# Weights' second part written by a negated copy and an adding DMA, in a four-layer mixer kernel on one core

## The chip, the core and the metric

The kernel runs on one core of a Trainium2 chip. The metric is the time of one execution on the device, in microseconds. The engines are named as the profile names them: PE (TensorE) multiplies matrices, PEld is its weight load, DVE (VectorE) and ACT (ScalarE) work elementwise, POOL (GpSimd) does so too and issues DMAs of its own, SP (SyncE) issues most DMAs.

## The reference, cut to what matters

The input is x, 512 tokens of 1024 features, in fp32. Four layers follow each other: a gated convolution of 31 taps beside an RWKV-7 recurrence; attention over keys that an indexer selects; an LRU; an attention with forget gates. Each begins and ends with large products of fp32 weights:

```python
z = h @ even_w_in[j]                      # 1024 x 7296
out = jnp.concatenate([ya, yb], axis=-1) @ even_w_out[j]   # 2048 x 1024
...
z = h @ odd_w_in[j]                       # 1024 x 4936
out = (o * jax.nn.silu(g)) @ odd_w_out[j] # 2048 x 1024
...
u = h @ w_in                              # LRU: 1024 x 3072, out 1536 x 1024
...
u = h @ w_in                              # forget gates: 1024 x 4112, out 1024 x 1024
```

The work between them is smaller on TensorE: the convolution, the recurrence in chunks of 64 tokens, the selection, two softmax attentions, the scan of the LRU.

## The kernel before, in words

Products are kept near fp32 by splitting both operands into two parts of the type fp32r, a first part h (the operand rounded) and a second part l (what rounding left). A product of one row tile (128 rows of the weights) is then three matmuls (`mm3`, L161 to L165): first part by first part (L163), first by second (L164), and the weights' second part by the first part of x (L165).

Weights come by column tiles of 128 columns. `wsplit` (L126) loads 8 row tiles of a column tile, 512 KB, through SP into `wr` (3 buffers), and makes the parts in two halves of 4 row tiles each: ScalarE casts the raw half into `wh` (L138), then GpSimd subtracts `wh` from the raw half into `wl` (L139). `wh` and `wl` have 4 buffers each, so a new half can be made when the half four back has been used. `wrows` (L143) does the same for rows of 7 column tiles in the first layer (L153, L154). In the LRU's output projection a half has 3 row tiles; in the last layer's products by tokens (`project_tok`) a half is one row tile of 512 columns, and two halves are used together. The last weights of all have buffers of their own (tag `pT`).

The convolution's taps are L835, `taps`: 27 products and sums on VectorE for each of 8 feature tiles, with some on GpSimd (L840). The inverse of the recurrence's triangular blocks is L665 and L666, 31 steps of a small product and a sum on VectorE. L870 sums the convolution's squares on GpSimd. The LRU's gates are functions on ScalarE (L1346 to L1361). L1088 is the one place where GpSimd issues DMAs: two copies of the indexer's keys from 64 partitions to the other 64.

The order on each engine is set by a scheduler that simulates the program as it is written; work marked as later is filled in behind. Each engine then works through its own queue in that order.

Of the kernel before, what the change touches and what calls it, by code (L numbers as in the profile page):

```python
# [10 lines left out]
F = mybir.dt.float32  # L11
R = mybir.dt.float32r
# [3 lines left out]
OP = mybir.AluOpType  # L16
# [15 lines left out]
# Columns of the packed vectors: a vector of n floats holds n / 128 columns.  # L32
# [20 lines left out]
class Ctx:  # L53
    """Pools, constants and the steps that the layers share."""
# [17 lines left out]
    @contextlib.contextmanager  # L72
    def layer(self, name, ps, **slots):
        """A pool for one layer's tiles: numbers of buffers by tag; for PSUM the banks, in turn."""
        self.slots, self.banks = slots, {tag: itertools.cycle(b) for tag, b in ps.items()}
        with self.tc.tile_pool(name=name, bufs=1) as self.sb:
            yield
# [6 lines left out]
    def one(self, name, shape, dt=F):  # L84
        """A tile of its own for the layer."""
        return self.sb.tile(list(shape), dt, name=self.name(name))
# [19 lines left out]
    def bias(self, v):  # L106
        """A column that holds v."""
# [17 lines left out]

    def wsplit(self, key, idx, k0, kn, rows=True, tag=None):  # L126
        """Rows k0 to k0 + kn (of 128) of a column tile of weights, each in two parts; or its halves."""
# [8 lines left out]
        for k in range(0, kn, n):  # L136
            h, l = (self.t(tag, (P, 4, P), R) if tag else self.wp.tile([P, 4, P], R, name=self.name(z), tag=z, bufs=4) for z in ("wh", "wl"))
            nc.scalar.copy(h[:, :n], raw[:, k:k + n])  # L138
            nc.gpsimd.tensor_tensor(out=l[:, :n], in0=raw[:, k:k + n], in1=h[:, :n].bitcast(F), op=OP.subtract)  # L139
            out += [(h[:, i], l[:, i]) for i in range(n)] if rows else [[z.rearrange("p a c -> p (a c)") for z in (h, l)]]  # L140
        return out

    def wrows(self, key, ct, k):  # L143
        """Rows k (of 128) of 7 or 8 column tiles, evenly apart, in two parts."""
# [5 lines left out]
        for o in (0, 4):  # L150
            m = min(4, n - o)
            h, l = (self.wp.tile([P, 4, P], R, name=self.name(z), tag=z, bufs=4) for z in ("wh", "wl"))
            nc.scalar.copy(h[:, :m], raw[:, o:o + m])  # L153
            nc.gpsimd.tensor_tensor(out=l[:, :m], in0=raw[:, o:o + m], in1=h[:, :m].bitcast(F), op=OP.subtract)  # L154
# [12 lines left out]
    def project(self, key, ct, xs, evac, group=1, sub=(), first=0, tag="mm"):  # L167
        """Column tiles ct of the weights, from row tile first on, times xs, a list of (h, l) of 128 rows."""
# [16 lines left out]
    def fill(self, key, ct, xs, evac, sub=()):  # L185
        """As project, a step of the sums at a time."""
# [11 lines left out]
    def lead(self, key, ct, xs, evac, tag="mm", sub=()):  # L198
        """As project, of two column tiles at once, a step of the sums of both at a time."""
# [10 lines left out]
    def steps(self, gen, n=None, after=None):  # L210
        """n steps, or all that are left, of work that fills gaps of TensorE: issued after an instruction."""
# [4 lines left out]
    def sums(self, key, ct, v, tag, raw):  # L216
        """Columns: column tiles ct of the weights times the vector v, 1024 long."""
# [17 lines left out]
    def project_halves(self, key, ct, xs, evac, tags, sub=()):  # L235
        """As project, the first half of xs for all column tiles first, then the first tokens: the rest comes later."""
# [15 lines left out]
    def project_tok(self, key, xs, evac, last=None):  # L252
        """xs as the stationary side: the result is by tokens. Weights by halves of the columns. A step at a time.
        last: a tag for the last weights, with which the last columns' blocks of tokens end one after the other."""
# [18 lines left out]
    def split(self, src, tag, scale=None):  # L273
        """src (fp32, SBUF or PSUM), times scale, as two fp32r tiles."""
# [15 lines left out]

    def bcast_tok(self, r, tag, dtag="s"):
        """r: [128 tokens, 4 blocks] -> [128, 512] in PSUM, the same in every partition."""
# [7 lines left out]
    def later(self, *after):  # L300
        """Work that fills gaps: yields to what is traced after it, and is issued after those instructions."""
# [12 lines left out]
    def stack(self, f, out, l=None):  # L314
        """Two heads of 64 rows, each split: both parts in the rows of a tile; or l, and the first part twice."""
# [8 lines left out]
    def shifted(self, f, shift):  # L324
        """f + shift, split."""
# [6 lines left out]
class SumSq:  # L332
    """Sums over the features of (x * g)^2, as the tiles of x come; by tokens in the end."""
# [26 lines left out]
def rms_cols(K, s):  # L360
    """1 / sqrt(s / 1024 + eps) by tokens."""
# [6 lines left out]
def log1p_exp_neg(K, t, bufs):  # L368
    """log(1 + exp(-t)) for t >= 0, by the series of atanh: t is overwritten."""
# [15 lines left out]
# ---------------------------------------------------------------- modulation  # L385


class Ada:
    """silu(c) @ ada_w[l] + ada_b[l], as columns: shift, scale and gate are 8 of them each."""
# [6 lines left out]
    def part(self, j, n, tags, after=None, acc="awa", ps="ada"):  # L396
        """Columns of 128, n of them from j on: returns what ends the sums."""
# [22 lines left out]
    def scale(self, j, n=4):  # L420
        """The norm's weight times 1 + scale, n columns."""
# [3 lines left out]
    def columns(self, i, tag):  # L425
        """Columns i and i + 1 of the shift and of the scale."""
# [21 lines left out]
# ---------------------------------------------------------------- layer 0: convolution and RWKV-7  # L448


def even_layer(K, ada1):
# [12 lines left out]
    with K.layer("even", {"mm": (0, 1), "t": (2, 3, 4), "u": (5, 6), "ada": (7,), "py": (7,)}, s=6, k=4, v=4, q4=3, no=1, Yt=1, BKt=2, SAV=2, U=3, cu=2, fg=3, mean=2, awa=1, pa=1):  # L464
# [11 lines left out]
        # a column tile of each kind, as the rows of h come  # L476
# [30 lines left out]
        # sigmoid(z) = (tanh(z / 2) + 1) / 2  # L507
# [3 lines left out]
        # the convolution is of 2 val sigmoid(glu): its norm undoes the 2  # L511
# [12 lines left out]
        def lora(ft, j):  # L524
            """tanh of half of the low-rank sums: 0 the decay's, 1 a's."""
# [6 lines left out]
        def head_sums(sqs, f, n=S):  # L532
            """f of the sums over each head's features, of 4 tiles of n tokens: [two parts of 8 heads, n]."""
# [20 lines left out]
        class Half:  # L554
            """8 heads."""
# [1074 lines left out]
```

## Time and profile before

| | us |
|---|---|
| runs | 1833.74, 1842.38, 1839.56 |
| median | 1839.56 |
| span of the profiled execution | 1835.4 |
| PE busy | 1685.5 (92%) |
| DVE busy | 1319.1 (72%) |
| ACT busy | 899.9 (49%) |
| POOL busy | 866.9 (47%) |
| DMA engines | 30.1% of the span for SP's queue, 1.1% for ACT's, 0.1% for POOL's |

The span runs from the first instruction to the last; what lies around it in that execution is not shown by the profile. Busy time is the time in which at least one instruction of an engine ran; matmuls overlap each other, so a busy PE may still be able to start them more closely. "Idle before" is the engine's idle time just ahead of an instruction, with the instruction that ended it.

### The profile page before, as it was taken

How to read it: one execution, taken by the hardware profiler on the slowest of the kernel's cores; microseconds unless marked ns; L12 is line 12 of the kernel's file. 1: busy time of each engine (PE TensorE's matmuls, PEld its weight loads, DVE VectorE, ACT ScalarE, POOL GpSimd, SP SyncE). 2: the span in 40 equal slices, each digit the busy share in tenths (PEclk: the TensorE clock that was granted, in tenths of full speed). 3: DMA queues.
4: the chain of work that ended last, by engine and by line, in shares of the span. 5: the costliest groups of instructions: out<-in, count | busy, mean ns of one | idle time of the engine just before them, and what ended most of it. 6: DMA issues, size and time to landing. Idle time of an engine off the chain costs nothing.

```text
span 1835.4 us, 25614 instructions
## 1 busy us (share of the span) xinstructions
PE 1685.5 (92%) x9250; PEld 1311.0 (71%) x9250; DVE 1319.1 (72%) x2246; ACT 899.9 (49%) x1699; POOL 866.9 (47%) x682
## 2 busy tenths in 40 slices
PE   3997889999895999898999999999988899999998
PEld 2765678776664777765778788888766687776776
DVE  6689997897969786568969978734898721455552
ACT  2443234334333524466344677644767633555564
POOL 4555564444585422354435555344544443444343
PEclk9997898998988889999999999999999999999999
DMA  9412352214243852331225310022222233321211
GB/s 271 131 58 69 118 144 72 83 47 135 78 126 120 266 185 97 97 99 58 92 86 169 119 53 13 24 92 92 81 89 66 78 103 108 104 81 61 81 55 70
DMA packets 111055, 182.15 MB, mean 99 GB/s; under 512 B 37296, under 2 KB 57136, under 8 KB 110928
## 3 DMA queue, kind: packets, MB, share of 16 engines
q1 hardware_dynamic: 106736, 172.91, 30.1%
q10 hardware_dynamic: 4032, 7.34, 1.1%
q8 instruction: 73, 1.20, 0.3%
q14 instruction: 54, 0.44, 0.1%
q0 software_dynamic: 160, 0.26, 0.1%
HBM read 162.10 MB, written 18.12 MB: 98 GB/s over the span
## 4 chain that ended last, share of the span: by engine, by line
PE 58%; DVE 32%; ACT 4%; issue 4%; DMA 2%; SPq 0%; POOL 0%; DVEq 0%; ACTq 0%
PE ps L163 15%; PE ps L164 15%; PE ps L165 14%; DVE x L835 7%; DVE q L665 2%; DVE xc L1300 2%; DVE q L666 2%; PE ps L1494 1%; DVE SAV L438 1%; DVE u L1369 1%; PE ps L706 1%; PE ps L1477 1%; PE ps L1490 1%; PE ps L1238 1%; PE ps L538 1%
## 5 line engine op out<-in xcount | busy, mean ns | idle before, releaser
L139 POOL TENSOR_TENSOR wl<-wr,wh 128x512 fp32r<-128x512 f32 (+1 forms) x400 | 563.6, 1413 | 657.1 <-ACT wh L138 614.3
L163 PE MATMUL ps<-h,wh 128*128 128x512 f32 x1240 | 511.2, 416 | 31.2 <-DVE s L516 13.2
L165 PE MATMUL ps<-h,wl 128*128 128x512 f32 x1240 | 505.7, 408 | 6.0 <-POOL wl L139 6.0
L164 PE MATMUL ps<-h,wh 128*128 128x512 f32 x1240 | 506.2, 408 | 3.2 <-DVE h L328 2.7
L138 ACT CAST wh<-wr 128x512 fp32r<-128x512 f32 (+1 forms) x400 | 242.0, 609 | 409.4 <-PE ps L164 332.4
L163 PEld LDWEIGHTS ps<-h,wh 128*128 128x128 f32 x1240 | 244.5, 197 | 98.8 <-DVE s L516 17.0
L165 PEld LDWEIGHTS ps<-h,wl 128*128 128x128 f32 x1240 | 243.5, 196 | 63.0 <-POOL wl L139 7.1
L164 PEld LDWEIGHTS ps<-h,wh 128*128 128x128 f32 x1240 | 244.0, 197 | 57.2 <-issue 3.6
L835 DVE SCALAR_TENSOR_TENSOR x<-cu,vec,x 128x512 f32<-128x512 f32 x216 | 214.5, 995 | 4.7
L1235 POOL TENSOR_SCALAR pp<-pp,st 128x512 f32<-128x512 f32 x32 | 52.3, 1634 | 51.9 <-DVE st L1231 38.3
L1484 DVE CUSTOM_DVE_ANT_0 pp<-ps,nb 128x128 f32<-128x128 f32 (+3 forms) x64 | 30.8, 488 | 42.4 <-PE ps L1479 31.2
L1230 ACT ACTIVATE pp<-pp,st 128x512 f32<-128x512 f32 x64 | 46.3, 723 | 23.8 <-DVE st L1229 23.6
L665 DVE TENSOR_TENSOR q<-q,q 128x112 f32<-128x112 f32 (+25 forms) x108 | 46.1, 461 | 15.0 <-POOL q L657 11.7
L1487 POOL TENSOR_SCALAR pp<-pp,st 128x128 f32<-128x128 f32 (+1 forms) x32 | 31.4, 986 | 47.9 <-DVE st L1486 47.8
L1229 DVE CUSTOM_DVE_ANT_0 pp<-ps,bias 128x512 f32<-128x512 f32 x64 | 43.4, 679 | 6.2 <-PE ps L1238 4.2
L164 PE MATMUL ps<-wl,h 128*128 128x512 f32 x120 | 47.2, 393 | 0.0
L1485 ACT ACTIVATE pp<-pp,st 128x128 f32<-128x128 f32 (+3 forms) x64 | 35.9, 561 | 21.8 <-DVE st L1484 21.3
L163 PE MATMUL ps<-wh,h 128*128 128x512 f32 x120 | 46.5, 403 | 0.0
L165 PE MATMUL ps<-wh,h 128*128 128x512 f32 x120 | 46.5, 393 | 0.0
L1491 ACT COPY pT<-ps 128x128 f32<-128x128 f32 (+3 forms) x64 | 26.6, 423 | 39.6 <-PE ps L1490 38.8
L284 DVE TENSOR_TENSOR pT<-ps,pT 128x512 fp32r<-128x512 f32 x64 | 43.4, 680 | 2.3 <-ACT pT L283 2.1
L283 ACT CAST pT<-ps 128x512 fp32r<-128x512 f32 x64 | 36.6, 577 | 16.2 <-PE ps L1238 15.7
(522 smaller groups left out, 3480.7 us busy)
## 6 DMA issues: line engine op xcount, KB each, us to landing
wr<-in_even_w_in SPq DMA_DIRECT2D x50, 512.0 KB, 3.5
wr<-in_odd_w_in SPq DMA_DIRECT2D x39, 512.0 KB, 3.5
wr<-in_lru_w_in SPq DMA_DIRECT2D x24, 512.0 KB, 3.4
wr<-in_fox_w_qkg SPq DMA_DIRECT2D x24, 512.0 KB, 3.5
k<-in_ada_w SPq DMA_DIRECT2D x32, 256.0 KB, 3.0
wr<-in_odd_w_out SPq DMA_DIRECT2D x16, 512.0 KB, 3.8
wr<-in_lru_w_out SPq DMA_DIRECT2D x16, 384.0 KB, 3.1
AR<-in_ada_w SPq DMA_DIRECT2D x4, 1024.0 KB, 9.8
```

Of the source, the lines that this page charges most:

```text
L138: nc.scalar.copy(h[:, :n], raw[:, k:k + n])
L139: nc.gpsimd.tensor_tensor(out=l[:, :n], in0=raw[:, k:k + n], in1=h[:, :n].bitcast(F), op=OP.subtract)
L163: mm(ps, lhsT=w[0], rhs=x[0], start=first, stop=False)
L164: mm(ps, lhsT=w[0], rhs=x[1], start=False, stop=False)
L165: self.last_mm = mm(ps, lhsT=w[1], rhs=x[0], start=False, stop=last).ins
L284: nc.vector.tensor_tensor(out=l, in0=src, in1=h.bitcast(F), op=OP.subtract)
L665: eng.tensor_tensor(out=z, in0=Yu[:, a, b:b + 1].to_broadcast(sh), in1=Nu[:, b:b + 1, b + 1:].to_broadcast(sh), op=OP.mult)
L666: eng.tensor_tensor(out=Yu[:, a, b + 1:], in0=Yu[:, a, b + 1:], in1=z, op=OP.add)
L835: nc.vector.scalar_tensor_tensor(out=acc, in0=u[:, q:q + S], scalar=w[q], in1=acc, op0=OP.mult, op1=OP.add)
L1229: nc.vector.tensor_tensor_reduce(out=pp, in0=lg, in1=bias[t], scale=1.0, scalar=3e38, op0=OP.add, op1=OP.min, accum_out=mx)
L1230: nc.scalar.activation(pp, pp, AF.Exp, scale=-1.0, bias=mx, accum_out=sm)
L1235: (nc.vector if t % 2 else nc.gpsimd).tensor_scalar(out=pp, in0=pp, scalar1=sm, scalar2=None, op0=OP.mult)
```

## The change

A half's second part is no longer subtracted by GpSimd. ScalarE writes the raw half a second time, times -1, into `wl`, which rounds it to fp32r as the first part was rounded; then a DMA from GpSimd's queue adds the raw half to it, in SBUF. `wl` then holds the raw value less the first part, as before. Both `wsplit` and `wrows` call the new function. 418 halves are made in this way (400 by L139 and 16 by L154 before, and 2 with the tag `pT`). The small weights of the LRU's gates (L1339) and the split of activations stay as they were. Comments and docstrings are dropped elsewhere, by which lines after L157 have a number higher by 5.

```diff
-            h, l = (self.t(tag, (P, 4, P), R) if tag else self.wp.tile([P, 4, P], R, name=self.name(z), tag=z, bufs=4) for z in ("wh", "wl"))
-            nc.scalar.copy(h[:, :n], raw[:, k:k + n])
-            nc.gpsimd.tensor_tensor(out=l[:, :n], in0=raw[:, k:k + n], in1=h[:, :n].bitcast(F), op=OP.subtract)
+            h, l = self.wparts(raw[:, k:k + n], tag)
...
+    def wparts(self, raw, tag=None):
+
+        nc, n = self.nc, raw.shape[1]
+        h, l = ((self.t(tag, (P, 4, P), R) if tag else self.wp.tile([P, 4, P], R, name=self.name(z), tag=z, bufs=4))[:, :n] for z in ("wh", "wl"))
+        nc.scalar.copy(h, raw)
+        nc.scalar.mul(l, raw, -1.0)
+        nc.gpsimd.dma_start(out=l, in_=raw, accum_op=OP.add)
+        return h, l
...
-            h, l = (self.wp.tile([P, 4, P], R, name=self.name(z), tag=z, bufs=4) for z in ("wh", "wl"))
-            nc.scalar.copy(h[:, :m], raw[:, o:o + m])
-            nc.gpsimd.tensor_tensor(out=l[:, :m], in0=raw[:, o:o + m], in1=h[:, :m].bitcast(F), op=OP.subtract)
+            h, l = self.wparts(raw[:, o:o + m])
```

GpSimd's queue where the convolution's squares are summed (`mean`, L870, L875 after the change) and the recurrence's inverse begins on VectorE; `wl`, `wh` and `wr` are the parts and the raw weights. Before:

```order
L870 TENSOR_TENSOR mean_4337<-mean_4337,cu_4348 128x512
L139 TENSOR_TENSOR wl_4492<-wr_4485,wh_4491 128x512
L870 TENSOR_TENSOR mean_4337<-mean_4337,cu_4352 128x512
L139 TENSOR_TENSOR wl_4527<-wr_4524,wh_4526 128x512
L870 TENSOR_TENSOR mean_4337<-mean_4337,cu_4356 128x512
L139 TENSOR_TENSOR wl_4531<-wr_4524,wh_4530 128x512
```

And after the change:

```order
L875 TENSOR_TENSOR mean_4441<-mean_4441,cu_4452 128x512
L147 DMA wl_4603<-wr_4595 128x512
L875 TENSOR_TENSOR mean_4441<-mean_4441,cu_4456 128x512
L147 DMA wl_4639<-wr_4636 128x512
L875 TENSOR_TENSOR mean_4441<-mean_4441,cu_4460 128x512
L147 DMA wl_4644<-wr_4636 128x512
```

Each subtraction has become a DMA in the same place; the sums between them have not moved.

ScalarE's queue in the LRU, between the functions of two feature tiles (L1346 to L1353 before, L1351 to L1358 after; `ri`, `u` and `m` are the gates' values). Before:

```order
L138 CAST wh_11841<-wr_11835 128x512
L138 CAST wh_11909<-wr_11907 128x512
L1346 ACTIVATE ri_11623<-ps_11619,hb_11425 128x512
L1338 CAST wah_11883<-wax_11881 128x256
L1346 ACTIVATE ri_11629<-ps_11625,hb_11425 128x512
L1351 ACTIVATE u_11631<-ri_11623,sp_11393 128x512
L283 CAST xs_11721<-xc_11714 128x512
L1352 ACTIVATE ri_11623<-ri_11623,sp_11394 128x512
L138 CAST wh_11913<-wr_11907 128x512
L1353 ACTIVATE m_11632<-ri_11623 128x512
```

And after the change:

```order
L1351 ACTIVATE ri_11891<-ps_11887,hb_11687 128x512
L1343 CAST wah_12159<-wax_12157 128x256
L1351 ACTIVATE ri_11897<-ps_11893,hb_11687 128x512
L145 CAST wh_12185<-wr_12183 128x512
L1356 ACTIVATE u_11899<-ri_11891,sp_11655 128x512
L146 ACTIVATE wl_12186<-wr_12183 128x512
L288 CAST xs_11993<-xc_11986 128x512
L1357 ACTIVATE ri_11891<-ri_11891,sp_11656 128x512
L145 CAST wh_12190<-wr_12183 128x512
L146 ACTIVATE wl_12191<-wr_12183 128x512
L1366 ACTIVATE g_12059<-f_12060 128x512
L1358 ACTIVATE m_11900<-ri_11891 128x512
```

A product (L146) follows each cast (L145) by one place or two, so it stands between the gates' functions where there was nothing or a cast alone.

## Rows read from the trace of the kernel before

**Rows 1.** Page, busy us (share of span) xinstructions.

```profile
PE 1685.5 (92%) x9250; PEld 1311.0 (71%) x9250; DVE 1319.1 (72%) x2246; ACT 899.9 (49%) x1699; POOL 866.9 (47%) x682
```

**Rows 2.** Page, costliest groups: busy, mean ns | idle before, releaser.

```profile
L139 POOL TENSOR_TENSOR wl<-wr,wh 128x512 fp32r<-128x512 f32 (+1 forms) x400 | 563.6, 1413 | 657.1 <-ACT wh L138 614.3
...
L138 ACT CAST wh<-wr 128x512 fp32r<-128x512 f32 (+1 forms) x400 | 242.0, 609 | 409.4 <-PE ps L164 332.4
...
L835 DVE SCALAR_TENSOR_TENSOR x<-cu,vec,x 128x512 f32<-128x512 f32 x216 | 214.5, 995 | 4.7
```

**Rows 3.** Chain of waits, 548 to 566 us: start, us, what.

```profile
548.73 0.23 PE ps L163
```

**Rows 4.** Timeline, ScalarE's casts, 549 to 556 us.

```profile
551.94 0.62 ACT L138 CAST wh<-wr 128x512 fp32r<-128x512 f32 x1 [0.50 <-PE ps L164]
...
554.66 0.63 ACT L138 CAST wh<-wr 128x512 fp32r<-128x512 f32 x1 [0.71 <-PE ps L164]
```

**Rows 5.** Waits: us in total, times, longest us.

```profile
ACT wh L138 <- PE ps L164: 332.4, 177, 10.0
...
PE ps L165 <- POOL wl L139: 6.3, 3, 5.4
```

**Rows 6.** Windows: busy us of each engine, granted clock, DMA share, GB/s.

```profile
0.00:50.00 50.00, 21.92 (x76) 16.72 (x76) 34.55 (x48) 13.51 (x22) 24.62 (x24) 1.00 0.92 278
450.00:500.00 50.00, 44.70 (x156) 31.67 (x157) 48.24 (x51) 20.50 (x33) 28.86 (x23) 0.87 0.32 95
1400.00:1450.00 50.00, 44.14 (x187) 34.08 (x185) 39.88 (x45) 36.40 (x56) 19.87 (x18) 1.00 0.20 59
1500.00:1550.00 50.00, 50.00 (x238) 39.84 (x238) 12.00 (x36) 17.58 (x29) 20.64 (x17) 1.00 0.33 109
```

**Rows 7.** Chain of waits, taps, 460 to 480 us.

```profile
466.55 0.76 DVE x L835
...
467.33 1.67 DVE x L835
```

**Rows 8.** Line L835: count, ns min/median/max, first and last start.

```profile
L835 DVE SCALAR_TENSOR_TENSOR x<-cu,vec,x x216: 721/752/1826, 83.0 to 516.6; 128x512 f32<-128x512 f32 x108
```

**Rows 9.** Timeline, GpSimd in the same stretch.

```profile
468.40 1.74 POOL L139 TENSOR_TENSOR wl<-wr,wh 128x512 fp32r<-128x512 f32 x1
```

**Rows 10.** Chain of waits, the inverse's start, 548 to 566 us.

```profile
549.59 13.81 DVE q L665 x2
```

**Rows 11.** Timeline, GpSimd beside it.

```profile
549.48 1.29 POOL L870 TENSOR_TENSOR mean<-mean,cu 128x512 f32<-128x512 f32 x1
550.73 1.30 POOL L139 TENSOR_TENSOR wl<-wr,wh 128x512 fp32r<-128x512 f32 x1
```

**Rows 12.** Chain of waits, first and last of the 120 long pieces.

```profile
21.09 1.65 DVE SAV L438
...
1451.72 1.33 DVE u L1370
```

**Rows 13.** Line L286: a tile times a number, as fp32r.

```profile
L286 ACT ACTIVATE qs<-s x16: 617/632/649, 849.3 to 1149.9; 128x512 fp32r<-128x512 f32 x16
```

**Rows 14.** Tile ki: GpSimd's DMAs, issue ns and landing us.

```profile
L1088 POOL DMA_DIRECT2D ki<-ki x2: 517/632/747, 805.7 to 806.9; - x2
...
DMA to landing us min/median/max: 2.2/2.3/2.4
```

**Rows 15.** Timeline, 803 to 812 us: GpSimd's issue and VectorE beside it.

```profile
805.73 0.75 POOL L1088 DMA_DIRECT2D ki<-ki  x1 [2.87 <-ACT ki L283]
...
805.96 0.68 DVE L284 TENSOR_TENSOR ki<-s,ki 64x512 fp32r<-64x512 f32 x1
```

**Rows 16.** Page, DMA queues: packets, MB, share of 16 engines.

```profile
q10 hardware_dynamic: 4032, 7.34, 1.1%
...
q0 software_dynamic: 160, 0.26, 0.1%
```

**Rows 17.** Windows, line L139 alone.

```profile
1500.00:1550.00 50.00, 20.64 (x17) 1.00 0.33 109
```

## The prediction

> **What bounds the kernel now.** I read the page's shares first: PE is busy 92% of the span [rows 1]. Then the groups of lines: some 400 weight halves are prepared by a ScalarE cast of 609 ns and a GpSimd subtraction of 1413 ns [rows 2]. A half is four row tiles, so 12 matmuls; where the weights stream, TensorE starts one each 0.23 us [rows 3] and the casts follow each other 2.72 us apart (551.94, 554.66) [rows 4]: 12 x 0.23 = 2.76 us is one half's time. That is the pace any new way of making a half has to keep. The waits say that preparation is not late today: the casts wait 332.4 us for TensorE to free a first-part buffer, and TensorE waits 6.3 us for a second part [rows 5].
>
> Where TensorE is not the bound, VectorE is: 48.24 of 50 us in 450 to 500, with PE at 44.70 [rows 6]. The chain of waits shows why. One convolution tap takes 0.76 us, the next one of the same shape 1.67 [rows 7]; over all 216 taps the least is 721 ns, the median 752, the most 1826 [rows 8]: two kinds, not a spread. In the same microseconds GpSimd ran a subtraction of 1.74 us [rows 9] against a mean of 1413. Two engines that read two SBUF operands each take turns. The extreme case is at 549.59, where two small products last 13.81 us [rows 10] while GpSimd goes from one operation to the next without a gap [rows 11]. Laying GpSimd's timeline beside the chain, I count 120 pieces of VectorE that run over 0.2 us longer than their undisturbed twins (0.72 to 0.76 us for a whole tile) while a weight subtraction is GpSimd's main work: the first at 21.09, the last at 1451.72 [rows 12]. Their excess adds up to 123 us of the chain, 13 of it from [rows 10].
>
> **The change part by part.**
> *Removed:* 400 subtractions, 563.6 us of GpSimd [rows 2], and 16 like them in the first 75 us. The end does not wait for GpSimd's time as such; what counts is the 123 us of turns on the chain. Not all come back. GpSimd's other operations also read SBUF (L870 alternates with L139 in [rows 11]) and keep their turns, and in 450 to 500 TensorE has only 50 - 44.70 = 5.3 us idle to give, although its low starts there can close up too. Ends: 0 and 123; I take 55, a little under half.
>
> *Added on ScalarE:* 418 products with -1. The row nearest is a whole tile times a number, written as fp32r: 632 ns [rows 13]. 418 x 0.63 = 264 us, so ScalarE goes from 49% to about 63%. In a stream that is 0.62 + 0.63 of 2.76 us, beside TensorE. It costs where ScalarE is full: in 1400 to 1450 it is busy 36.40 us [rows 6], with some 15 halves 36.4 + 15 x 0.63 = 46 of 50. The order there puts the products between the gates' functions; each such function is late by up to 0.63 us, and the product waits one matmul longer (0.23) for its buffer than the cast did. Ends 0 and 20 us; I take 5.
>
> *Added on GpSimd's queue:* 418 DMAs. The only ones that the trace has move 64 rows of 2 KB: 517 to 747 ns to issue and 2.3 us to landing [rows 14]. 128 rows and a second operand may make it two to four times as long: 1.0 to 3.0 us, I take 1.5, about what the subtraction took, so GpSimd's queue is as occupied as before and what stands behind a DMA there (L870, L1235) is no later. VectorE's two-operand instruction beside that issue took 0.68 us, undisturbed [rows 15]; so I count no turns for a DMA's issue.
>
> *Landing.* Before, a second part was ready 1.4 us after its cast. Now: 0.63 for the product, then the DMA. From 2.3 us for 128 KB I estimate 3.4 us for 256 KB read twice (2.3 us as the lower end, 6 us under load as the upper). With a wait for ScalarE the path from a freed buffer to a ready one is about 5 us, at worst 8. Four buffers rotate, so a freed one is needed three halves later: 3 x 2.76 = 8.3 us. That is hidden in the column projections. It is not where the rotation is short: the by-token projections use two halves together (16 pairs, 5.5 us apart), and the LRU's output has halves of three row tiles (32, three of them 6.2 us). At 0.5 us a pair and 0.3 us a half that is 18 us; I take 15, between 0 and 40.
>
> *DMA engines.* The ACT queue's row gives a price per packet: 1.1% of 16 x 1835.4 us over 4032 packets is 80 ns at 1.8 KB [rows 16]. One plain DMA of 128 rows has 144 packets by the existing pair (160 for two of 64 rows): 144 x 80 / 16 = 0.72 us of all engines; with two reads for each write 1.44. The software queue's own row, 0.1% (0.05 to 0.15 by rounding) for 160 packets, reaches 275 ns and so 5.0 us. I take 1.44, since the 80 ns come from 4032 packets. In 1500 to 1550 the engines are busy 0.33 [rows 6], 0.91 us a half; 0.91 + 1.44 = 2.35 of 2.76 us. It fits, narrowly. At the start they are at 0.92: 8 DMAs (the parts of the first four loads) at 1.44 us, 11.5 us, do not fit in the 4 us left, of which I charge 5 (0 to 15).
>
> The Trainium skill, "DMA: Bandwidth & Descriptors", section "Anatomy of one DMA — SWDGE (gpsimd) path", states 2.0 us plus the bytes over 436 GB/s. That would be 2.6 us by its figures; the 2.3 us row agrees for 128 KB, and with 2.6 the 15 us for short rotations would go, leaving 1795. Against the change speaks the skill's page "SBUF — State Buffer", section "SBUF: two separate sides": while VectorE runs a mode that takes both ports, GpSimd cannot write descriptors. No row here has a GpSimd DMA beside such an operation; by that rule each could wait one of them out, some tenths of a us, within the landing's ends above.
>
> *Sum:* 55 gained, 5 + 15 + 5 = 25 lost: -30. The profiled execution has a span of 1835.4 us, and no more of its time is shown; 1835.4 - 30 = 1805.4. The three runs' median is 1839.56, 4.2 above that span, so the forecast is **1810 us**.
>
> **Rivals.**
> *A, the accumulating DMA does not keep the pace.* The point: more than 2.76 - 0.91 = 1.85 us of all engines for each. For it: the 5.0 us end, and a margin of only 0.4 us; against it: 80 ns a packet. From 1500 to 1550 there are 17 halves [rows 17]; the stretches like it (850 to 1000, 1200 to 1600) hold, by my estimate at that density or a little under, some 200. At 2.3 us they are 0.45 us short each, 90 us: 1839.6 - 30 + 90 = 1900; at 1.85 and a bit, with lateness alone, 1850; at 3.3 us 0.91 + 3.3 = 4.2 for 2.76, +290, about 2100. The place is TensorE at the third product of a row tile (L165 before, L170 after), which would wait for second parts, with DMA at nine tenths.
> *B, no change.* The turns go, but TensorE was next and the chain moves to it; for it speaks the 92%. Then 123 us shrink to about 25, the charges eat them: 1840 (1830 to 1849).
> *C, the turns come back whole* and the charges are hidden by the buffers: 1839.6 - 85 = 1755. For it: TensorE's starts at 0.23 us leave it more room than its busy share says (156 matmuls in 450 to 500 need 36 us); against it: GpSimd's other operations keep taking turns.
>
> **How the numbers follow.** Forecast (1785 to 1830) 0.44; C and what lies below 1785 0.08; B 0.14; A 0.34, of which 0.12 above 1915. Half a per cent, 9 us, is about what runs of this kernel can tell from no change. Faster 0.52, same 0.14, slower 0.34. The forecast's own range is 1785 to 1830; A's part up to 1915 has to be in the 8 of 10: 1785 to 1915.
>
> **What would show it.** Right: the taps' mean falls from 995 towards 800 ns, and the two products at 549.59 from 13.81 to a few us; ScalarE's busy time is near 1160 us; TensorE's waits for a second part stay below 40 us in all; landing of the new DMAs has a median under 5 us. Wrong: landing above 8 us or an issue above 2.7 us, TensorE idle before that third product by 100 us or more, DMA at 9 tenths in the projections (A); taps as fast as I say with the total unmoved (B).

## The result, and the profile after

The changed kernel takes 1806.72 us (median of four runs, 1806.24 to 1814.26) against 1836.94 for the kernel before, measured beside it: a ratio of 0.9845 with a 95% interval of 0.9817 to 0.9873. The forecast was 1810 us. By the medians the kernel gained 30.2 us, and 30 were forecast; the forecast lies 3 us higher because it was worked out from the 1839.56 us of three runs. The profiled execution is the slowest of the four: 1814.26 us with a span of 1812.5. It is 8 us above the other three, so a stage read from one execution is uncertain by about that much.

The page of the changed kernel: busy time and share of each engine, then three DMA queues (packets, MB, share of 16 engines), then the chain that ended last (the run of work and waits, followed back from the last instruction), by engine; the last row is that chain before the change.

```profile
PE 1684.2 (93%) x9250; PEld 1306.3 (72%) x9250; DVE 1140.0 (63%) x2246; ACT 1102.2 (61%) x2117; POOL 643.0 (35%) x682
...
q0 software_dynamic: 60352, 107.24, 35.0%
q1 hardware_dynamic: 106736, 172.91, 30.8%
q10 hardware_dynamic: 4032, 7.34, 1.1%
...
PE 62%; DVE 13%; DMA 10%; issue 6%; ACT 6%; POOL 2%; SPq 0%; POOLq 0%; ACTq 0%; DVEq 0%
...
PE 58%; DVE 32%; ACT 4%; issue 4%; DMA 2%; SPq 0%; POOL 0%; DVEq 0%; ACTq 0%
```

Beside [rows 1], VectorE lost 179 us of busy time (1319.1 to 1140.0) with the same 2246 instructions. TensorE's busy time stayed (1685.5 to 1684.2). Its idle time, span less busy, fell from 149.9 to 128.3 us: that is nearly all of what the span lost. In the chain VectorE went from 32% to 13% and DMA from 2% to 10%, so a good part of what VectorE gave back went to transfers.

Costliest groups of the changed kernel: busy, mean ns | idle before, releaser.

```profile
L147 POOL DMA_DIRECT2D wl<-wr x416 | 365.9, 887 | 884.9 <-ACT wl L146 771.9
...
L146 ACT ACTIVATE wl<-wr 128x512 fp32r<-128x512 f32 (+1 forms) x416 | 256.6, 617 | 34.9 <-PE ps L169 28.1
L840 DVE SCALAR_TENSOR_TENSOR x<-cu,vec,x 128x512 f32<-128x512 f32 x216 | 178.0, 827 | 4.5
```

A tap takes 827 ns in the mean, 995 in [rows 2]. The next answers are for single lines: count, ns min/median/max, first and last start; for the DMA also its landing; then VectorE's timeline at the place of [rows 10], GpSimd's beside it, and TensorE's behind it.

```profile
L147 POOL DMA_DIRECT2D wl<-wr x416: 830/860/1699, 21.1 to 1792.2; - x139
DMA to landing us min/median/max: 3.0/4.2/8.2
L840 DVE SCALAR_TENSOR_TENSOR x<-cu,vec,x x216: 723/752/2205, 87.6 to 492.1; 128x512 f32<-128x512 f32 x108
...
527.13 0.57 DVE L670 TENSOR_TENSOR q<-q,q 128x31 f32<-128x31 f32 x2 [13.43 <-DMA q<-sp]
...
530.62 13.29 POOL L875 TENSOR_TENSOR mean<-mean,cu 128x512 f32<-128x512 f32 x1
...
548.94 0.80 PE L170 MATMUL ps<-h,wl 128*128 128x512 f32 x1 [10.01 <-DMA wl<-wr]
```

The two small products that lasted 13.81 us now last 0.57. But the collision has not gone: it has turned around. VectorE now goes from one step of the inverse to the next without a gap, and one of GpSimd's sums (L875), 1.29 us long in [rows 11], takes 13.29. The adding DMA behind that sum in GpSimd's queue starts only at 543.85, and TensorE sits idle for 10.01 us until it has landed. The taps still have a largest value of 2205 ns: two taps that begin at 390.54 take 3.13 us together, with two of GpSimd's own operations (L852, L845) beside them, so its other work goes on taking turns with VectorE. Waits of the changed kernel: us in total, times, longest us; the last two rows are of SyncE's queue, which loads the weights, after and before the change.

```profile
PE ps L170 <- DMA wl<-wr: 28.4, 20, 10.0
...
SPq L133 <- DMA wl<-wr: 1204.4, 193, 48.0
...
SPq L133 <- POOL wl L139: 1114.9, 183, 49.9
```

Where [rows 5] had 6.3 us, TensorE's matmuls now wait 28.4 us for a second part; the longest of these waits, 10.0 us, is the one at 548.94. The last rows show something more: a load of weights (L133) now waits until the adding DMA has read the raw tile, where GpSimd's subtraction freed it before. These waits grew by 90 us in all; what that cost isn't shown.

Windows of the changed kernel: busy us of each engine, granted clock, DMA share, GB/s. Then pieces of its chain of waits: start, us, what.

```profile
0.00:50.00 50.00, 18.80 (x74) 15.13 (x75) 32.96 (x48) 16.84 (x29) 17.68 (x23) 1.00 0.96 277
450.00:500.00 50.00, 47.33 (x197) 32.43 (x196) 47.35 (x60) 27.07 (x47) 27.14 (x30) 0.93 0.72 168
540.00:545.00 5.00, 0.00 (x0) 0.00 (x0) 5.00 (x19) 0.00 (x0) 5.00 (x3) 0.84 0.05 4
550.00:600.00 50.00, 43.06 (x386) 33.73 (x385) 25.74 (x36) 29.51 (x51) 18.41 (x19) 0.83 0.99 265
1500.00:1550.00 50.00, 50.00 (x247) 39.95 (x246) 13.23 (x46) 30.25 (x58) 15.00 (x18) 1.00 0.87 204
```

```profile
232.81 7.30 DMA wl<-wr
...
530.62 13.24 POOL mean L875
543.85 5.04 DMA wl<-wr
...
770.54 5.84 DMA wl<-wr
```

In the even stream of 1500 to 1550 TensorE is full beside a DMA share of 0.87. The losses stand elsewhere: at the start, where TensorE is busy for 18.80 us instead of the 21.92 of [rows 6], at 232.81 and in the second layer's input products (770.54). The one at 543.85 is not the work of many transfers: from 540 to 545 TensorE does nothing while the DMA engines' share is 0.05, because the DMA's issue stands behind GpSimd's long sum. The share of 0.99 comes after it.

Where the span goes by stage, from one execution of each kernel. The marks are the first starts of lines 862, 1298 and 1401 of the kernel before (867, 1303 and 1406 after): the convolution's mean, the LRU, the last layer. The experiments e1 and so on come below.

| kernel | to L862 | to L1298 | to L1401 | to the end | span |
|---|---|---|---|---|---|
| before | 528 | 751 | 246 | 310 | 1835.4 |
| after | 504 | 756 | 239 | 314 | 1812.5 |
| e1 GpSimd only writes | 467 | 726 | 224 | 308 | 1724.8 |
| e5 plain DMA, no product | 479 | 735 | 226 | 308 | 1747.1 |
| e3 plain DMA | 479 | 734 | 237 | 309 | 1759.2 |
| e11 e3 and traffic | 501 | 759 | 241 | 309 | 1811.0 |
| e9 e3 and delay | 509 | 756 | 252 | 315 | 1831.4 |

The change gained 24 us before L862 and 7 in the LRU, and lost 5 between and 5 at the end; of these only the 24 is clear of the 8 us between executions.

### The profile page after: what moved, and what is told of

The parts are those of the page before. It is cut to its first block, busy times and chain, and to the rows that moved or that the text cites. A ratio compares the mean times of both kernels' runs of the same rounds, so it can differ in the third digit from the quotient of the medians.

```text
span 1812.5 us, 26549 instructions
## 1 busy us (share of the span) xinstructions
PE 1684.2 (93%) x9250; PEld 1306.3 (72%) x9250; DVE 1140.0 (63%) x2246; ACT 1102.2 (61%) x2117; POOL 643.0 (35%) x682
## 4 chain that ended last, share of the span: by engine, by line
PE 62%; DVE 13%; DMA 10%; issue 6%; ACT 6%; POOL 2%; SPq 0%; POOLq 0%; ACTq 0%; DVEq 0%
PE ps L168 16%; PE ps L170 16%; PE ps L169 16%; DMA wl<-wr 3%; DVE x L840 2%; PE ps L711 1%; DMA adm<-in_ada_w 1%; PE ps L1499 1%; DVE SAV L443 1%; PE ps L1482 1%; ACT wl L146 1%; PE ps L1495 1%; POOL wl L147 1%; PE ps L1243 1%; DMA wr<-in_even_w_in 1%
## 5 line engine op out<-in xcount | busy, mean ns | idle before, releaser
L147 POOL DMA_DIRECT2D wl<-wr x416 | 365.9, 887 | 884.9 <-ACT wl L146 771.9
L170 PE MATMUL ps<-h,wl 128*128 128x512 f32 x1240 | 499.5, 408 | 26.1 <-DMA wl<-wr 25.5
L168 PE MATMUL ps<-h,wh 128*128 128x512 f32 x1240 | 508.2, 414 | 10.3 <-ACT h L288 3.4
L169 PE MATMUL ps<-h,wh 128*128 128x512 f32 x1240 | 497.7, 404 | 0.0
L145 ACT CAST wh<-wr 128x512 fp32r<-128x512 f32 (+1 forms) x416 | 251.8, 605 | 331.3 <-PE ps L169 237.5
L168 PEld LDWEIGHTS ps<-h,wh 128*128 128x128 f32 x1240 | 241.8, 195 | 74.9 <-issue 6.3
L169 PEld LDWEIGHTS ps<-h,wh 128*128 128x128 f32 x1240 | 241.2, 195 | 53.2 <-issue 4.5
L146 ACT ACTIVATE wl<-wr 128x512 fp32r<-128x512 f32 (+1 forms) x416 | 256.6, 617 | 34.9 <-PE ps L169 28.1
L840 DVE SCALAR_TENSOR_TENSOR x<-cu,vec,x 128x512 f32<-128x512 f32 x216 | 178.0, 827 | 4.5
```

What stands on the lines that cost most here:

```text
L145: nc.scalar.copy(h, raw)
L146: nc.scalar.mul(l, raw, -1.0)
L147: nc.gpsimd.dma_start(out=l, in_=raw, accum_op=OP.add)
L168: mm(ps, lhsT=w[0], rhs=x[0], start=first, stop=False)
L169: mm(ps, lhsT=w[0], rhs=x[1], start=False, stop=False)
L170: self.last_mm = mm(ps, lhsT=w[1], rhs=x[0], start=False, stop=last).ins
```

## The experiments

A turn here is the time that VectorE loses to a GpSimd operation beside it. The theory at the start: the turns of GpSimd's subtraction were worth some 55 us, and the new way of making a second part gives back 25. Its rivals: the gain is GpSimd's shorter queue and not the turns; the price is ScalarE's product, or the DMA. Times are medians, with the ratio to the kernel before on the same chip and its interval; that kernel took 1836.9 to 1838.8 us.

**e1, GpSimd only writes** (kernel before; the subtraction is left out at both of its places, the second part is zero).

```diff
-nc.gpsimd.tensor_tensor(out=l[:, :n], in0=raw[:, k:k + n], in1=h[:, :n].bitcast(F), op=OP.subtract)
+for _ in range(3):
+    nc.gpsimd.memset(l[:, :n].bitcast(F), 0.0)
```

> The kernel before, but GpSimd only writes each weight half's second part (three memsets of zero in a row in place of the subtraction; the second part's product is therefore left out of the result). GpSimd stays occupied for about as long (3 x 0.5 us against 1.41), but reads nothing from SBUF; no DMA is added, ScalarE has no second product. Theory of the turns (two engines that read two SBUF operands each alternate): VectorE's taps fall from 995 ns towards 827 or less, VectorE's busy time to about 1140 us as in the changed kernel, and the time to 1836.9 - 50 = about 1787 us, lower than the changed kernel's 1806.7 because nothing of the change's price is paid. Rival, that the gain comes from a shorter stay in GpSimd's queue: no change, 1828 to 1846 us. Rival, that it comes from a new order of the schedule: anything, with VectorE's busy time unmoved at 1319.

Measured: 1724.64 us, 0.9386 [0.9361, 0.9412]. I expected 1787. Page and groups of this kernel:

```profile
PE 1646.8 (95%) x9250; PEld 1292.6 (75%) x9250; DVE 1142.6 (66%) x2246; ACT 902.2 (52%) x1699; POOL 930.6 (54%) x1518
...
L140 POOL MEMSET wl<- 128x512 f32 (+1 forms) x1200 | 621.7, 525 | 519.7 <-PE ps L167 444.3
L837 DVE SCALAR_TENSOR_TENSOR x<-cu,vec,x 128x512 f32<-128x512 f32 x216 | 180.2, 837 | 4.4
```

GpSimd is busier than before (930.6 against 866.9 us), and still 112 us are gone, with the taps at 837 ns. So the queue theory falls: it is the reading, and the turns cost up to twice what I took. One thing else changes in e1: a write waits neither for the load nor for the cast, but for TensorE (the releaser in its row). In e2 the wait for the cast stays.

**e2, one operand read** (kernel before; GpSimd copies the first part, so the second part is not the remainder).

```diff
-nc.gpsimd.tensor_tensor(out=l[:, :n], in0=raw[:, k:k + n], in1=h[:, :n].bitcast(F), op=OP.subtract)
+nc.gpsimd.tensor_copy(l[:, :n], h[:, :n].bitcast(F))
```

> The kernel before, but GpSimd copies the first part to the second part (one SBUF operand read and one write; the subtraction is left out of the result). If any GpSimd operation that reads SBUF makes VectorE's two-operand instructions take turns: VectorE's taps stay near 950 to 1000 ns where they meet, though each turn is shorter if the copy is shorter than 1.41 us (at about 0.8 us the excess falls by 40%), and the time is between 1800 and 1836, about 1815 us. If only two-operand GpSimd operations take turns: taps near 827, as with memsets, about 1787 us.

Measured: 1752.03 us, 0.9551 [0.9525, 0.9577]. I expected about 1815.

```profile
L139 POOL CAST wl<-wh 128x512 fp32r<-128x512 f32 (+1 forms) x400 | 301.2, 755 | 762.6 <-ACT wh L138 703.1
L835 DVE SCALAR_TENSOR_TENSOR x<-cu,vec,x 128x512 f32<-128x512 f32 x216 | 190.6, 884 | 4.6
```

With one operand read the taps stand at 884 ns, between 837 and 995, and 27 of the 112 us come back: one operand makes turns as well, but fewer; the copies also take only 301.2 us of GpSimd where the subtractions took 563.6. The copy waits for its cast as the subtraction did, and still 85 us are gone. So neither e1's earlier writes nor e2's shorter copies can be the whole cause: e2 is without the first, e1 without the second, and what the two have in common is that GpSimd reads less.

**e3, a plain DMA** (changed kernel without the addition: the second part is the raw weights).

```diff
-nc.gpsimd.dma_start(out=l, in_=raw, accum_op=OP.add)
+nc.gpsimd.dma_start(out=l, in_=raw)
```

> The changed kernel, but the DMA copies the raw half over the second part and does not add (the second part is therefore the raw half in the result). It measures what adding costs: two reads for each write. If the price goes by reads: software queue's share 35% falls to about 17%, 0.76 us of all engines each, landing from 4.2 to about 3 us, and of the 22 to 25 us that the change gives back (start 4.6, first layer's output 8.5 and second layer's start 4.5, second layer's attention 7) about half return: 1795 us. If the price of a DMA lies in its descriptors and its fixed latency: share and landing barely move, 1804 to 1809 us.

Measured: 1766.48 us, 0.9631 [0.9588, 0.9675]. Group, landing and queue of this kernel:

```profile
L147 POOL DMA_DIRECT2D wl<-wr x416 | 229.1, 551 | 940.9 <-ACT wl L146 852.8
...
DMA to landing us min/median/max: 2.1/2.7/6.8
...
q0 software_dynamic: 60352, 107.24, 20.2%
```

I expected 1795, or 1804 to 1809. So adding costs 40 us over copying: 0.34 us more to issue, 1.5 us later to land, and 0.67 us more of all 16 engines (35.0% of 1812.5 against 20.2% of 1759.2, over 418 DMAs: 1.52 against 0.85).

**e4, a hybrid** (DMA for the column tiles of the first layer's and the LRU's input products, the subtraction elsewhere).

```diff
+h, l = self.wparts(raw[:, k:k + n], tag, key in ("even_w_in", "lru_w_in_2"))
...
+if dma:
+    nc.scalar.mul(l, raw, -1.0)
+    nc.gpsimd.dma_start(out=l, in_=raw, accum_op=OP.add)
+else:
+    nc.gpsimd.tensor_tensor(out=l, in0=raw, in1=h.bitcast(F), op=OP.subtract)
```

> The DMA only for the input projections of the first layer and of the LRU, where the gains were (38 us up to 594 us of the span, 12 us in the LRU), the subtraction on GpSimd everywhere else and for the loads of the first 75 us. Theory: gains stay, the losses elsewhere go: 1836.9 - 50 = about 1787 us, with milestones at or before the changed kernel's at every stage (the second layer's selection begins about 783 us into the span, before: 820, changed: 797). Rival, that the losses of the changed kernel are the schedule's own and not the DMA's: 1800 to 1810 us.

Measured: 1788.82 us, 0.9741 [0.9708, 0.9773]. It beats both kernels; the intervals of the two ratios don't meet. Its profile has 506 us to L862 as the changed one, and 744 and 308 in the other two stages in which the changed kernel had lost (756 and 314).

**e5, plain DMA, no product** (e3 without ScalarE's product; the second part is the raw weights).

```diff
-nc.scalar.mul(l, raw, -1.0)
 nc.gpsimd.dma_start(out=l, in_=raw)
```

> The changed kernel with a plain copying DMA (as in the run before it, 1766.48 us) and also without ScalarE's product, so that the second part is the raw weights. It prices the product alone. If ScalarE's 416 x 0.617 us lie beside other work, as the prediction says (cost 5 us): 1758 to 1766 us. If the product stands in each chain from load to second part, and ScalarE, busy 63%, makes TensorE wait: 1730 to 1750 us, most of the 42 us that the plain DMA still costs beside the kernel in which GpSimd only writes (1724.64 us). I expect the first, about 1760.

Measured: 1748.67 us, 0.9502 [0.9477, 0.9526]. I expected 1760. The product costs 18 us by the medians. The table, with e3's fastest execution and e5's slowest, has 12 of them, all in the LRU. In 1310 to 1360, in the LRU, TensorE is busy for 45.69 us with the product and for all 50 without, at nearly the same ScalarE time of 44.76 and 44.11 us (first and fourth engine columns; e3, then e5):

```profile
1310.00:1360.00 50.00, 45.69 (x194) 35.32 (x193) 36.47 (x53) 44.76 (x73) 10.65 (x20) 1.00 0.45 135
```

```profile
1310.00:1360.00 50.00, 50.00 (x220) 41.00 (x219) 39.59 (x58) 44.11 (x68) 11.11 (x22) 1.00 0.56 159
```

**e6, more traffic** (changed kernel with a DMA of each half's raw weights to DRAM on GpSimd's queue).

```diff
 nc.gpsimd.dma_start(out=l, in_=raw, accum_op=OP.add)
+nc.gpsimd.dma_start(out=d[:, :n], in_=raw)
```

> The changed kernel with a second, plain GpSimd-queue DMA of 256 KB for each half, from the raw weights into DRAM that nobody reads. By rival A, in which the 16 DMA engines set the pace: to 1.52 us for the adding DMA and about 1.3 for loads per half come some 0.85, 3.7 us together against TensorE's 2.76, so in the stretches with DMA share above 0.85 the time grows by a fifth or more: 1860 to 2050 us, the first 500 us above all. If only the landing of one DMA matters and the engines have room: 1807 to 1825 us. In between, 1830 to 1860, it is the order within the queue and not the engines' sum. I expect 1900, since shares of 0.90 to 0.99 stand in the first 250 us and at 550 to 600 us already.

Measured: 1992.13 us, 1.0839 [1.0811, 1.0867]. The DMA engines seem to have little to spare; but the order within GpSimd's queue changes too, and its new DMAs wait for loads there. e11 adds work for the engines on another queue.

```profile
q0 software_dynamic: 93152, 214.23, 46.7%
...
POOL traf L151 <- DMA wr<-in_even_w_in: 166.7, 41, 9.1
```

**e7, half and half** (e4 with only the first half of each of those column tiles by DMA).

```diff
-key in ("even_w_in", "lru_w_in_2")
+key in ("even_w_in", "lru_w_in_2") and k == 0
```

> The hybrid (1788.82 us), in which of each column tile of the first layer's input products and the LRU's one half of the rows goes by the DMA and the other by GpSimd's subtraction. If turns and DMA engines cost in proportion: the first 528 us of before and 505 of the changed kernel give about 516 there, in all about 1795 to 1805 us. If each price is that of a queue that is nearly full, and halves of both leave both with room: under 1780 us. I expect 1785 to 1800.

Measured: 1816.34 us, 0.9867 [0.9834, 0.99], slower than the 1785 to 1800 that I expected: 21 of the hybrid's 48 us are left, which the interval doesn't tell from a half. Half of the subtractions bring back about half of the turns: the taps are at 934 ns between the hybrid's 848 and the 995 of before, (934 - 848) / (995 - 848) = 59% of the way (e7, then e4). To L862 it is still 19 us ahead of before (510 against 528), the hybrid 23; why the stage after it is slower (760 against 744) I can't say.

```profile
L843 DVE SCALAR_TENSOR_TENSOR x<-cu,vec,x 128x512 f32<-128x512 f32 x216 | 201.3, 934 | 4.6
...
L843 DVE SCALAR_TENSOR_TENSOR x<-cu,vec,x 128x512 f32<-128x512 f32 x216 | 182.6, 848 | 4.6
```

**e8, VectorE subtracts** (e4 with VectorE in GpSimd's place in the attention layers and the out-projections).

```diff
-nc.gpsimd.tensor_tensor(out=l, in0=raw, in1=h.bitcast(F), op=OP.subtract)
+(nc.vector if dve else nc.gpsimd).tensor_tensor(out=l, in0=raw, in1=h.bitcast(F), op=OP.subtract)
```

> The hybrid (1788.82 us) with VectorE in GpSimd's place for the subtraction in the attention layers, and in the out-projections, where VectorE is often idle: no turns of this kind are left there, and VectorE gets one instruction of some 0.7 us for each of about 250 halves. The two kernels in which GpSimd doesn't subtract passed the second layer's attention 26 us sooner than the kernel before. If VectorE's room holds the subtraction: 1765 to 1785 us. If the weights then queue behind VectorE's other work (43 to 48 of 50 us are busy at 850 to 1050 us): 1790 to 1815 us. I expect about 1780.

Measured: 1790.67 us, 0.9749 [0.9716, 0.9782]: no different from the hybrid. VectorE's busy time rises by 84 us (1219.8 to 1304.1) for 172.8 us of subtractions of its own, so some 88 us are gone elsewhere, which I read as turns that it no longer has.

```profile
L150 DVE TENSOR_TENSOR wl<-wr,wh 128x512 fp32r<-128x512 f32 (+1 forms) x252 | 172.8, 687 | 120.3 <-ACT wh L145 119.6
```

**e9, plain DMA, delayed** (e3 with GpSimd's three writes ahead of each DMA; the second part is the raw weights).

```diff
+for _ in range(3):
+    nc.gpsimd.memset(l.bitcast(F), 0.0)
 nc.gpsimd.dma_start(out=l, in_=raw)
```

> The kernel with the plain copying DMA (1766.48 us) and, ahead of each of these DMAs, three writes by GpSimd into the second part, some 3 x 0.525 = 1.57 us: about what the adding DMA needs more than the plain one (4.2 against 2.7 us to landing, 0.86 against 0.55 to issue), but with no more work for the 16 DMA engines. The second part is the raw weights. If the 40 us that adding costs come from the later landing and the longer issue: 1795 to 1815 us. If they come from the engines' work (1.52 us of all 16 per adding DMA against 0.85): 1760 to 1775 us. I expect about 1775, the engines the larger part, since the DMA share stood at 0.85 to 0.99 where the changed kernel lost.

Measured: 1834.12 us, 0.9987 [0.9971, 1.0003]. I expected 1775. Writes of 1.57 us ahead of each DMA cost 68 us with no more work for the DMA engines (landing 2.5 us in the median). The writes also keep GpSimd busy for 640.6 us, so some of it may be other work of GpSimd that comes later, and the run does not give the price of a later second part alone.

```profile
L148 POOL MEMSET wl<- 128x512 f32 (+1 forms) x1248 | 640.6, 523 | 424.6 <-ACT wl L146 363.4
...
DMA to landing us min/median/max: 2.1/2.5/7.2
```

**e10, traffic on SyncE's queue** (e3 and a copy of each weight tile from DRAM to DRAM; the second part is the raw weights).

```diff
 nc.sync.dma_start(out=raw[:, :kn], in_=self.ins[key][idx][:, k0:k0 + kn])
+nc.sync.dma_start(out=d[:, :kn], in_=self.ins[key][idx][:, k0:k0 + kn])
```

> The kernel with the plain copying DMA (1766.48 us) and, behind each load of weights, a second DMA on SyncE's queue that copies the same weights from DRAM to a place in DRAM that nobody reads: more work for the DMA engines, by some 0.65 to 0.85 us per half (which the share of queue q1 will tell), without a longer issue on GpSimd. The second part is the raw weights. If adding costs by the engines' work: 1795 to 1820 us. If by the adding DMA's own latency: 1766 to 1780 us. I expect about 1800.

Measured: 2084.45 us, 1.1354 [1.1332, 1.1377], which answers nothing: the copies wait for no buffer, and the scheduler put them ahead. The last layer's were issued at 160 to 368 us, and until then TensorE nearly stands still. Line of the copies, and the page's 40 slices of TensorE, its clock and the DMA engines:

```profile
L136 SPq DMA_DIRECT2D traf<-in_fox_w_qkg x24: 488/489/2147, 160.0 to 368.3; - x24
...
PE   3210110699899999699899999999999989999998
...
PEclk9555555799989989889999999999999999999999
DMA  9999999646932457775464567311655557654433
```

**e11, traffic on ScalarE's queue** (e3 and a DMA of each first part to DRAM, which has to wait for the cast; the second part is the raw weights).

```diff
 nc.gpsimd.dma_start(out=l, in_=raw)
+nc.scalar.dma_start(out=d[:, :n], in_=h.bitcast(F))
```

> The kernel with the plain copying DMA (1766.48 us) and, on ScalarE's own DMA queue, behind each cast, a DMA of 256 KB from the first part into DRAM that nobody reads: work for the DMA engines (the share of queue q10 will tell how much; 0.65 to 0.85 us of all 16 per half are expected, as much as adding costs over copying), with nothing more in GpSimd's queue or in the chain to the second part. The second part is the raw weights. If the DMA engines' work is what adding costs: 1795 to 1830 us. If it is the later landing and the longer issue, as the run with three writes ahead of the DMA says (1834 us by 1.57 us of delay): 1766 to 1785 us. I expect 1780.

Measured: 1811.71 us, 0.9840 [0.9812, 0.9867]. I expected 1780.

```profile
q10 hardware_dynamic: 64224, 114.32, 17.3%
...
L147 POOL DMA_DIRECT2D wl<-wr x416: 527/528/797, 20.3 to 1790.6; - x139
DMA to landing us min/median/max: 2.1/3.9/8.3
```

The new DMAs take (17.3 - 1.1)% of 1811.0 over 418, 0.70 us of all engines each: as much as adding over copying. The plain DMA is issued as fast as in e3 (528 ns), but lands at 3.9 us instead of 2.7, and the time rises by 45 us, in the same stages as from e3 to the changed kernel. In the chain, waits for a second part to land add up to 18 us in e3, 49 here and 62 in the changed kernel. So the engines' work can account for most of the 40 us, by making everything land later. But the run does not add that work alone: each new DMA also takes 326 ns of ScalarE's queue to issue, 136 us in all. At the product's price, 18 us for 257, that is an estimated 10 of the 45.

```profile
L150 ACTq DMA_DIRECT2D traf<-wh x416: 325/326/1211, 29.4 to 1790.9; - x139
```

Part of the price is clock. TensorE's busy time is 1660.2 us in e3 and 1685.3 here, as in the changed kernel (1684.2); the mean granted clock over the span is 0.972, 0.962 and 0.961 (rows of e3, then e11):

```profile
PE 1660.2 (94%) x9250; PEld 1295.7 (74%) x9250; DVE 1130.1 (64%) x2246; ACT 1103.3 (63%) x2117; POOL 510.0 (29%) x682
...
PE 1685.3 (93%) x9250; PEld 1307.9 (72%) x9250; DVE 1130.0 (62%) x2246; ACT 1104.4 (61%) x2117; POOL 513.6 (28%) x682
```

**e12, product first** (changed kernel, ScalarE's product and the DMA ahead of the cast).

```diff
-nc.scalar.copy(h, raw)
-nc.scalar.mul(l, raw, -1.0)
+m = nc.scalar.mul(l, raw, -1.0).ins
 nc.gpsimd.dma_start(out=l, in_=raw, accum_op=OP.add)
+with self.tc.issue_after(m):
+    nc.scalar.copy(h, raw)
```

> The changed kernel (1806.72 us) with ScalarE's product ahead of its cast in all 416 halves: the adding DMA can start 0.6 us sooner, the first part comes 0.6 us later, and nothing else differs. If the time from a load to its second part is what the change pays: the run with three writes cost 67.6 us for 1.57 us, 43 us per us, so 0.6 us sooner gives 26 us back: 1770 to 1795 us. If the DMA engines' work is what it pays, or the later first part costs as much: 1800 to 1830 us. I expect 1785.

Measured: 1801.57 us, 0.9798 [0.9755, 0.9841], which the intervals don't tell from the changed kernel. A second part 0.6 us sooner with a first part 0.6 us later gives 5 us by the medians and 9 by the ratios (0.9798 against 0.9845), not 26. The long sum of GpSimd isn't there in this kernel (its longest is 2.20 us), so what there is may come from that as well.

## Why the prediction was right, point by point

The account in measured steps from the kernel before: -112 for the turns (e1), +24 for a plain DMA in the place of GpSimd's writes (e1 to e5), +18 for the product (e5 to e3), +40 for adding (e3 to after): -30. Each is uncertain by some 5 to 10 us, and they add up to the whole by the way they are made. The forecast was -55 + 5 + 20 = -30. The direction and the kinds of cost were right; that the sum came out was luck. None of its terms was right: each was taken at between a quarter and a half, and the errors cancelled.

*What bounds the kernel.* Right: TensorE first and VectorE's turns in its gaps; the taps' mean fell to 827 ns (towards 800) and the two products of [rows 10] to 0.57 us. What it did not foresee is that GpSimd would then be the one that is held up there, for 13.29 us, on the chain. VectorE's 1140.0 us of busy time beside the 1142.6 of e1 bear out that a DMA's issue makes no turns to speak of.

*The turns' worth.* Mis-sized: 55 taken of 0 to 123, 112 measured in e1, 85 in e2. I discounted for GpSimd's other operations and for TensorE's small idle share. The first did not matter, since the count of 123 us was to hold only pieces beside weight subtractions. (The pair that I showed does not: the tap of [rows 7] ran from 467.33 to 469.00, and until 468.44 it was one of GpSimd's own sums, L840, that ran beside it; the subtraction of [rows 9] began at 468.40.) In the second I let TensorE's busy time give little. In e1 it fell from 1685.5 to 1646.8, with a mean granted clock of 0.977 against 0.955 over the span: 39 of the span's 111 us, a third of the gain, lie in TensorE's own matmuls, of which fewer ran at the lower level.

*ScalarE.* The product's 617 ns came as said ([rows 13]: 632 ns), and the place too, the LRU; 5 us taken, 18 measured, within the end of 20. ScalarE's busy time is 1102.2 us, not 1160: a cast and a product next to each other overlap (at 1508.37 a product of 0.63 us, at 1508.91 the cast behind it).

*Landing and DMA engines.* The issue was 0.86 us, below the range of 1.0 to 3.0; the landing was 4.2 us, not 3.4, within 2.3 to 6; the engines' work was 1.52 us per DMA, near the 1.44 from 80 ns a packet; and 1500 to 1550 stands at 0.87 where 2.35 of 2.76 gives 0.85. Yet 15 + 5 us were taken where 24 + 40 = 64 were paid. The step that failed is "It fits, narrowly": I let the engines cost nothing in a stream that has room and looked for a loss only at the start. e11 shows the price below full: more work makes every landing later, and the chain waits for it (18 us of landings in e3, 49 in e11, 62 in the changed kernel). Not all of the 64 is of that kind: the long sum of GpSimd is on the chain for 10.16 us in e5, 11.42 in e3 and 13.24 in the changed kernel, and only for 1.30 us in e1, where the sum itself is just as long (12.90). In GpSimd's queue I had counted how long each DMA occupies it, and not what stands ahead of it. Nor did the rotation argument count the raw weights' buffers, which are now held until the DMA has read them (1204.4 us of SyncE's waits against 1114.9). Whether a fourth raw buffer would give anything back is open.

*Against the Trainium skill.* By the Trainium skill's "DMA: Bandwidth & Descriptors", section "Anatomy of one DMA — SWDGE (gpsimd) path", 256 KB take an estimated 2.6 us. e3's plain DMA agrees with 2.7, the adding one does not with 4.2. The Trainium skill's "SBUF — State Buffer", section "SBUF: two separate sides", has GpSimd kept from writing descriptors while VectorE runs an operation in a mode that takes both ports. No run here shows what that cost. Of the 416 issues the least took 830 ns, the mean 887 and the longest 1699, so (887 - 830) x 416 = 24 us of longer issues, on an engine that is 65% idle, are the most that could be put down to it. How many of these stood beside such an operation isn't known.

*The rivals.* A did not come: 1.52 us is under its 1.85, and TensorE is full in the stream. What e3 and e11 show, work of the engines that makes second parts late, is its mechanism at a lower dose. B falls with e1. C's first half was true, the turns did come back nearly whole (its 1755 took 85 us for them; all 123 would have made 1717, and e1 came to 1725); its second, that the buffers hide the charges, was not.

What stays open: of the 40 us for adding, how much is the queueing for engines and how much the DMA's own latency and longer issue. e11 says that the first can be most of it, with ScalarE's issues mixed in; e9 that delay costs much as well, with GpSimd's busy time mixed in; e12 that 0.6 us sooner gives little back while the first part is later. No run takes the long sum of GpSimd out alone.

## What to carry to other kernels

Before moving an elementwise step to a DMA, price three things apart with kernels that leave the others out: what the removed reads cost (write only), what a plain copy costs, and what adding costs on top. DMA engines at shares of 0.7 to 0.9, as here, are not free: work on them was paid in later landings. Look also at what stands ahead of the new DMA in its queue: here one sum that VectorE held up made TensorE wait for 10 us. As far as these runs go, put such a DMA only where VectorE is the bound and the engines have room, and leave the old way elsewhere: the hybrid kept 148 of the 418 DMAs and was faster than either.

## What the runs showed of the hardware that was not expected

- GpSimd writing SBUF without reading it costs VectorE next to nothing: with 621.7 us of writes the taps are at 837 ns (827 in the changed kernel); with 301.2 us of reading one operand they are at 884, with 563.6 us of reading two at 995.
- Who is held up can change. Before, GpSimd ran without a gap and two small products of VectorE took 13.81 us; after, VectorE ran without a gap and one sum of GpSimd took 13.29 us.
- A DMA that adds takes 1.52 us of all engines for 256 KB against 0.85 for a copy, 860 ns to issue against 530, and lands at 4.2 us against 2.7.
- The turns also go with a lower clock: 0.955 granted over the span before, 0.977 in e1. In the chain of the changed kernel a long tap, for which TensorE waits, is followed by matmuls at 0.43 us, and then by matmuls at 0.23; the granted clock of 450 to 500 is 0.93:

```profile
489.09 1.14 DVE x L840
490.23 0.67 DVE s L521
...
495.15 0.43 PE ps L168
...
495.86 0.23 PE ps L170
```

0.43 us is the pace at 1.2 GHz (the granted clock is 0.50 in 545 to 550, where TensorE's three matmuls all start behind its long wait), and 0.23 us that at 2.4 GHz (1.00 in 1500 to 1550).
